# Expert results scattered to two DRAM rows per token, large tiles on multiples of 512 bytes, and a 4 KB descriptor ring

## The chip, the cores and the metric

The kernel runs on one core of a Trainium2 chip. The metric is the device time of one execution in microseconds. Three runs of the kernel before took 1555.31, 1557.9 and 1559.6 us, median 1557.9. A core has five engines that matter here: TensorE (PE; its weight loads are PEld), VectorE (DVE), ScalarE (ACT), GpSimd (POOL) and SyncE (SP), and 16 DMA engines that all queues share. SP and ACT issue plain transfers, GpSimd the indirect ones.

## The reference

Two transformer blocks run one after the other on x of 512 tokens by 1024. The first has a chunked mLSTM beside a convolution branch (glu) and a gated feed-forward net; the second has latent attention and retention, cross attention on a memory, and a mixture of 32 experts, which is what the change is about:

```python
hm = rms_norm_2(x, moe_norm_g)
g_sel = argmax(hm @ w_group + b_group)                 # one group of 8 experts per token
_, top_idx = lax.top_k(e_logits + e_bias, 2)           # two experts of it
act = silu(hm @ w_gate[e]) * (hm @ w_up[e]) * gate[:, e]
x = x + sum over e of act @ w_down[e]                  # gate is zero but for the two experts
```

Every token so has a first and a second expert, and 512 tokens make 1024 pieces of work. Each expert has 3 MB of weights (1024 x 512 and 256 x 1024 in float32), 100 MB in all.

## The kernel before

The phases follow each other, and a scheduler moves instructions of later phases ahead on each engine: mem (memory projections), glu, qk and vo with the mLSTM, wout, up and down (the feed-forward net), mlain, g, ret and att (second block), wout2, crossq, wo, and moe. A product in float32 is made of three matmuls on split operands (L146 to L148). Weight pieces of 512 KB come by SP into `raw` tiles (three buffers) and are split by ACT and DVE into `whl` tiles (four) (L131 to L141).

**The expert loop.** The 32 experts run as 16 pairs, p and p+16: the slots of the first are partitions 0 to 63, those of the second 64 to 127. So there are 2048 slots for 1024 pieces of work. `look` turns a pair's one-hot `oh` into the token of each slot and its gates by four small matmuls on `parts`; `fetch` (L1818) gathers the tokens' rows from `hd` in DRAM by an indirect DMA that drops unused slots; `pair_flip` (L1771) transposes them to `xT`; `pair_up` makes 16 matmuls (L1880), silu on ACT (L1882) and the product `sl` on DVE (L1883); `pair_turn` transposes `sl` to `aT` (L1891, L1893); `pair_down` (L1906) gives the result, which ACT and DVE copy into `yt` (L1912); `pair_scatter` (L1916) is an indirect DMA of GpSimd that adds `yt`'s 128 rows to `sums` in DRAM; unused slots go to spare rows at its end. `sums` was filled with x ahead of the loop (L1623, eight DMAs of ACT). After the loop SP reads `sums` into `xs` (tiles `crossq_U`, L1713), pair 15 is added by matmuls (`pair_last`, L1947, L1948) and SP stores the output (L1949, eight DMAs of 256 KB).

**The places.** The weights of the experts are 192 pieces of 512 KB (12 a pair). They are loaded by SP (L1755) into a ring of places, tiles that have become free: eight `ew`, four rows of X, two of `misc`, three `raw`, four `whl` twice, four rows of a U tile twice, and at last the four tiles of `xs`, 37 in all. Piece n goes to place n modulo 37 and so waits for piece n-37 to be used. The last four pieces are loaded as eight halves (L1749).

Of the kernel before, what the change touches and what calls it, by code (L numbers as in the profile page):

```python
# [46 lines left out]
class Kern:  # L47
# [15 lines left out]
    def setup(self):  # L63
# [11 lines left out]
        nc.vector.memset(self.half, -0.5)  # L75

# [419 lines left out]
    def block1(self):  # L496
# [47 lines left out]
        with tc.tile_pool(name="pf", bufs=1) as pf:  # L544
# [20 lines left out]
            self.rope_tables()  # L565
            g2row = self.mod_row(pf.tile([P, 1024], F32, tag="row1", name="g2row"), 2, 1, "ffn_post_g")
# [14 lines left out]
            for self.later in self.wide_product(act, "ffn_down", NFF, (((0, 1), 0, 8), ((0,), 8, 22), ((1,), 8, 22)),  # L581
                                                self.post(g2row, after)):
                pass

# [182 lines left out]
    def gate_cols(self, pa, gi, B, M):  # L767
# [6 lines left out]
        ac = pa.tile([P, 32], F32, tag="acol", name="acol")  # L774
        nc.vector.tensor_copy(ac, pt[:, :32])
# [216 lines left out]
    def attention(self, p2):  # L992
# [12 lines left out]
        sspe = p2.tile([P, 4], F32, tag="sspe", name="sspe")  # L1005

# [470 lines left out]
    def select_tiles(self, pm):  # L1477
# [3 lines left out]
        self.sel = {"oh": T("goh", 4), "o1": T("go1", 4, 8), "o2": T("go2", 4, 8), "mask": T("mask", 32), "mb": T("mb", 32, dt=BF16)}  # L1481
        self.pos = T("pos", 32)

    def select(self, pm, lg, br, t0, n):
# [19 lines left out]
        for dst in (s["mb"], s["mask"]):  # L1504
            nc.vector.tensor_tensor(dst[:, t].rearrange("p t (g e) -> p t g e", g=4), ob, ohb, op=ALU.mult)
# [51 lines left out]
    def moe(self, pm, o, X):  # L1557
# [27 lines left out]
        self.sums = self.dr.tile([S + P, D], F32, tag="sums", name="sums")  # L1585

# [6 lines left out]
        self.spare = pm.tile([P, 1], F32, tag="spare", name="spare")  # L1593
        nc.gpsimd.iota(self.spare, pattern=[[1, 1]], base=S - 1024, channel_multiplier=1, allow_small_or_imprecise_dtypes=True)
# [4 lines left out]
        def logits(tb, h):  # L1599
# [23 lines left out]
            nc.scalar.dma_start(self.sums[tb * P:(tb + 1) * P, c], x)  # L1623
# [23 lines left out]
        self.pieces = []  # L1647
# [5 lines left out]
        def route(tbs):  # L1653
            self.places_of(tbs)
            t = slice(tbs[0], tbs[-1] + 1)
            self.slots(oh[:, t], self.pair_pos(0)[:, t])
# [26 lines left out]
        for p in range(3):  # L1683
            st[p] = st.get(p, {})
            st[p]["oh"] = self.slots(self.slot_tile(), self.pair_pos(p))
# [5 lines left out]
        for p in range(3):  # L1691
            self.pair_gates(st[p], self.look(st[p]["oh"], self.parts), (p, p + 16, 32))
        nwin = self.more_windows(pm, mb, onb)

        xs = self.xs
        self.places += xs
        self.prefetch(0)
        yt = pm.tile([P, 2, 1024], F32, tag="y", name="yt")
        for i in range(16):
# [5 lines left out]
            if i + 3 < 16:  # L1705
                p = i + 3
                st[p] = self.pair_take(self.pair_pos(p), self.parts, (p, p + 16, 32))
# [13 lines left out]
    def places_early(self, X):  # L1721

        t = self.pm.tile([P, self.EXTRA, 1024], F32, tag="ew", name="ew")
        self.places = [t[:, i] for i in range(self.EXTRA)] + [X.rows(4 + i) for i in range(4)]
# [53 lines left out]
    def pair_pos(self, p):  # L1778

        return self.pos.rearrange("p t (j e) -> p t e j", j=2)[:, :, p]  # L1780
# [20 lines left out]
    def look(self, oh, parts):  # L1801
# [3 lines left out]
        o = ps[:, 0:3 * n].rearrange("p (n i) -> p n i", i=3)  # L1805
        for tb in range(4):
            self.nc.tensor.matmul(o, oh[:, tb].rearrange("p a b -> p (a b)"), parts[:, tb], start=tb == 0, stop=tb == 3)
# [13 lines left out]
    def pair_gates(self, s, ps, cols):  # L1821
# [8 lines left out]
        nc.vector.tensor_tensor(gt[:, 0:1], gt[:, 0:1], gt[:, 2:3], op=ALU.mult)  # L1830

        e = self.small(1)
# [5 lines left out]
    def pair_take(self, pos, parts, cols):  # L1838
# [306 lines left out]
```

## Time and profile before

| what | us |
|---|---|
| median of three runs | 1557.9 |
| lowest, highest | 1555.31, 1559.6 |
| profiled execution | 1556.0 |
| its span | 1554.3 |
| TensorE busy in the span | 1475.9 (95%) |
| VectorE, ScalarE, GpSimd busy | 947.2, 671.3, 132.4 |

Three kinds of view are used. The windows give the busy time of each engine in a stretch, the clock of TensorE and the share in which the 16 DMA engines had packets under way. The chain of waits leads from the last instruction back to what released each. The DMA view gives bytes, queues and the time from issue to landing of a stretch. A matmul's duration is longer than the distance from one to the next, since they overlap.

### The profile page before, as it was taken

The numbers are of one execution on the slowest core, as the hardware profiler recorded it, in microseconds if no ns is written. First come the engines' busy times: TensorE is split into PE (matmuls) and PEld (weight loads), VectorE is DVE, ScalarE is ACT, GpSimd is POOL, SyncE is SP. The second block draws the span as 40 slices with busy tenths as digits, with TensorE's granted clock in tenths as the row PEclk, the third lists the DMA queues.
The fourth block names the chain that finished last, engine by engine and source line by source line (L and its number), as shares of the span: only waits on it lengthen the run. The fifth ranks groups of instructions, "written<-read, shape, count | busy, mean of one in ns | idle before, by whom it ended". The sixth has DMA issues, their size and how long they took to land.

```text
span 1554.3 us, 19779 instructions
## 1 busy us (share of the span) xinstructions
PE 1475.9 (95%) x7032; PEld 1084.6 (70%) x7032; DVE 947.2 (61%) x2090; ACT 671.3 (43%) x1212; POOL 132.4 (9%) x153
## 2 busy tenths in 40 slices
PE   7989999999999999999999999999998999998886
PEld 4667778778888888888888877778877873332322
DVE  4568999985856865656525778766587565321112
ACT  4554586567746644444324554444355321110000
POOL 0111111011000000000000010100010002221100
PEclk9999999999999999999999999999999999999999
DMA  8899977876376433333435633342352689999997
GB/s 318 301 267 261 266 198 189 241 180 150 97 273 198 137 109 95 93 91 93 144 108 180 204 115 100 124 140 72 116 181 110 255 330 338 376 376 389 384 383 289
DMA packets 94470, 321.38 MB, mean 207 GB/s; under 512 B 12026, under 2 KB 12538, under 8 KB 94368
## 3 DMA queue, kind: packets, MB, share of 16 engines
q1 hardware_dynamic: 78384, 270.10, 50.1%
q0 software_dynamic: 11952, 39.49, 12.1%
q10 hardware_dynamic: 4032, 10.49, 1.8%
q8 instruction: 57, 0.93, 0.2%
q14 instruction: 45, 0.37, 0.1%
HBM read 273.74 MB, written 24.64 MB: 192 GB/s over the span
## 4 chain that ended last, share of the span: by engine, by line
PE 67%; DMA 16%; DVE 10%; ACT 2%; issue 2%; POOL 2%; SPq 0%; DVEq 0%; ACTq 0%; POOLq 0%
PE up_pa L148 5%; PE up_pa L147 5%; PE up_pa L146 5%; DMA ew<-in_w_gu_dram 3%; PE moe_pa L1880 2%; DVE y L632 2%; PE vo_pa L146 2%; PE vo_pa L148 2%; PE vo_pa L147 2%; PE wout_pa L148 2%; DMA moe_ew<-in_w_gu_dram 2%; PE wout_pa L146 2%; PE wout_pa L147 2%; DMA glu_raw<-in_w_in_dram 2%; DMA crossq_U<-in_w_dn_dram 2%
## 5 line engine op out<-in xcount | busy, mean ns | idle before, releaser
L632 DVE SCALAR_TENSOR_TENSOR y<-g,cols,y 128x493 f32<-128x493 f32 (+26 forms) x240 | 165.6, 727 | 6.6 <-ACT y L629 4.9
L148 PE MATMUL up_pa<-u,up_w 128*128 128x512 f32 (+1 forms) x384 | 145.6, 380 | 0.0
L147 PE MATMUL up_pa<-u,up_w 128*128 128x512 f32 (+1 forms) x384 | 144.1, 376 | 0.5 <-DVE u L189 0.5
L146 PE MATMUL up_pa<-u,up_w 128*128 128x512 f32 (+1 forms) x384 | 144.3, 377 | 0.0
L919 DVE SCALAR_TENSOR_TENSOR up_tA<-up_pa,cols,up_tA 128x511 f32<-128x511 f32 x88 | 65.8, 748 | 78.7 <-ACT up_tA L917 77.3
L1772 DVE COPY moe_xT<-moe_pb 128x512 f32<-128x512 f32 x15 | 10.4, 692 | 124.3 <-PE moe_pa L1880 122.8
L147 PEld LDWEIGHTS up_pa<-u,up_w 128*128 128x128 f32 x384 | 72.1, 188 | 16.6 <-DVE u L189 0.8
L146 PEld LDWEIGHTS up_pa<-u,up_w 128*128 128x128 f32 x384 | 72.4, 189 | 15.2 <-ACT u L188 0.5
L148 PEld LDWEIGHTS up_pa<-u,up_w 128*128 128x128 f32 x384 | 72.2, 188 | 13.8
L141 DVE TENSOR_TENSOR down_w<-down_raw,down_w 128x1024 fp32r<-128x1024 f32 x36 | 42.7, 1219 | 56.0 <-ACT down_w L135 56.0
L141 DVE TENSOR_TENSOR wout_w<-wout_raw,wout_w 128x512 fp32r<-128x512 f32 (+1 forms) x72 | 51.3, 745 | 35.2 <-ACT wout_w L135 35.1
L1882 ACT ACTIVATE moe_sl<-moe_pa,moe_gt 128x256 f32<-128x256 f32 x16 | 7.6, 473 | 141.6 <-PE moe_pa L1880 141.6
L917 ACT ACTIVATE up_tA<-up_pa,cols 128x512 f32<-128x512 f32 x44 | 34.2, 778 | 73.4 <-PE up_pa L148 73.4
L135 ACT CAST down_w<-down_raw 128x1024 fp32r<-128x1024 f32 x36 | 36.6, 1050 | 64.9 <-PE down_pb L148 31.9
L135 ACT CAST wout_w<-wout_raw 128x512 fp32r<-128x512 f32 (+1 forms) x72 | 44.9, 670 | 44.3 <-PE wout_pa L148 22.0
L146 PE MATMUL glu_pa<-mem_U,glu_w 128*128 128x512 f32 x128 | 51.1, 402 | 4.4 <-ACT mem_U L188 4.4
L141 DVE TENSOR_TENSOR up_w<-up_raw,up_w 128x1024 fp32r<-128x1024 f32 (+1 forms) x48 | 54.0, 1126 | 0.1
L147 PE MATMUL g_pa<-g_w,down_U 128*128 128x512 f32 x128 | 51.0, 398 | 0.5 <-DVE g_w L141 0.5
L146 PE MATMUL g_pa<-g_w,down_U 128*128 128x512 f32 x128 | 51.4, 402 | 0.0
L147 PE MATMUL glu_pa<-mem_U,glu_w 128*128 128x512 f32 x128 | 50.5, 396 | 0.4 <-DVE mem_U L189 0.4
L148 PE MATMUL g_pa<-g_w,down_U 128*128 128x512 f32 x128 | 50.7, 396 | 0.0
L148 PE MATMUL glu_pa<-mem_U,glu_w 128*128 128x512 f32 x128 | 50.4, 395 | 0.0
(749 smaller groups left out, 3944.4 us busy)
## 6 DMA issues: line engine op xcount, KB each, us to landing
up_raw<-in_ffn_up_dram SPq DMA_DIRECT2D x44, 512.0 KB, 3.5
wout_raw<-in_w_out_dram SPq DMA_DIRECT2D x40, 512.0 KB, 4.2
down_raw<-in_ffn_down_dram SPq DMA_DIRECT2D x36, 512.0 KB, 3.7
ew<-in_w_gu_dram SPq DMA_DIRECT2D x33, 512.0 KB, 10.0
glu_U<-in_ada_w_dram SPq DMA_DIRECT2D x32, 512.0 KB, 8.1
crossq_U<-in_w_gu_dram SPq DMA_DIRECT2D x24, 512.0 KB, 12.3
moe_ew<-in_w_gu_dram SPq DMA_DIRECT2D x19, 512.0 KB, 13.2
mem_raw<-in_w_kv_dram SPq DMA_DIRECT2D x16, 512.0 KB, 6.1
```

The lines of the kernel that those rows point to most:

```text
L135: nc.scalar.copy(w[:, 0, c], raw[:, c])
L141: nc.vector.tensor_tensor(w[:, 1, c], raw[:, c], w[:, 0, c].bitcast(F32), op=ALU.subtract)
L146: mm(out, lh, rh, start=start, stop=False)
L147: mm(out, lh, rl, start=False, stop=False)
L148: mm(out, ll, rh, start=False, stop=stop)
L632: nc.vector.scalar_tensor_tensor(acc[:, s:], g[:, :512 - s], cw[:, j:j + 1], acc[:, s:], op0=ALU.mult, op1=ALU.add)
L917: nc.scalar.activation(acc, pq, AF.Identity, scale=cwv(2), bias=self.col("ffn_conv_b", cc))
L919: nc.vector.scalar_tensor_tensor(acc[:, s:], pq[:, :512 - s], cwv(2 - s), acc[:, s:], op0=ALU.mult, op1=ALU.add)
L1772: (nc.scalar.copy if i else nc.vector.tensor_copy)(t[:, i * 4:i * 4 + 4].rearrange("p k c -> p (k c)"), ps)
L1880: nc.tensor.matmul(ps[r, :], s["xT"][:, k, r], w[j][k // 2][:, (k % 2) * 512:(k % 2 + 1) * 512], start=k == 0, stop=k == 7)
L1882: nc.scalar.activation(sl, ps[:, :256], AF.Silu, scale=s["gt"][:, 2:3])
```

## The change

It has five parts.

- The scatter no longer adds. Each pair's `yt` goes to `rows`, 1024 rows of 4 KB: row t for a token's first expert, row 512 + t for its second. Unused slots are dropped. To know which it is, `select` keeps a one-hot `second`, and `look` multiplies it with `oh` in four more matmuls. Pair 15 is added by matmuls as before.
- `clear_rows` writes zeros to all of `rows`: one memset and 16 DMAs of 256 KB on SP. They are placed in the up phase.
- x is no longer written to `sums`; it stays in `xs`, whose tiles are no places any more. A new tile `early` gives two places that are filled in glu. So there are 35.
- After pair 14 ACT issues eight DMAs of 512 KB that read `rows` into places, and eight adds of 128x1024 on VectorE add them to `xs`.
- Unused tiles (`gap0`, `gapa`, `gap2`, `gap`) are put between tiles so that large ones start at a multiple of 512 bytes in a partition; the ring of descriptors for GpSimd's DMAs goes from 16 to 4 KB a partition, which makes the room. Of the tiles in the prediction `u`, `up_act` and `mT` move from 352 past a multiple to a multiple; `ew` starts off one before (352) and after (480); the U tiles, `raw` and `whl` tiles are on one in both.

```diff
+        self.p0.tile([P, 112], F32, tag="gap0", name="gap0")
...
             self.rope_tables()
+            self.clear_rows()
...
+        self.rows = self.dr.tile([2 * S, D], F32, tag="rows", name="rows")
+        z = self.tB()
+        nc.vector.memset(z, 0.0)
+        for i in range(8):
+            for h in range(2):
+                nc.sync.dma_start(self.rows[i * P:(i + 1) * P, h * 512:(h + 1) * 512], z)
...
+        early = self.p0.tile([P, 2, 1024], F32, tag="early", name="early")
+        self.pieces, self.places = [], [early[:, 0], early[:, 1]]
+        self.prefetch(0)
...
-        for dst in (s["mb"], s["mask"]):
-            nc.vector.tensor_tensor(dst[:, t].rearrange("p t (g e) -> p t g e", g=4), ob, ohb, op=ALU.mult)
+        for dst, v in (("mb", ob), ("mask", ob), ("second", o2)):
+            nc.vector.tensor_tensor(s[dst][:, t].rearrange("p t (g e) -> p t g e", g=4), v, ohb, op=ALU.mult)
...
-            nc.scalar.dma_start(self.sums[tb * P:(tb + 1) * P, c], x)
...
-        self.places += xs
-        self.prefetch(0)
...
+            if i == 14:
+                n = len(self.places)
+                for tb in range(4):
+                    for k in range(2):
+                        z = self.places[(192 + 2 * tb + k) % n]
+                        nc.scalar.dma_start(z, self.rows[k * S + tb * P:k * S + (tb + 1) * P, :])
         for tb in range(4):
-            nc.sync.dma_start(xs[tb], self.sums[tb * P:(tb + 1) * P, :])
+            for k in range(2):
+                z = self.places[(192 + 2 * tb + k) % n]
+                nc.vector.tensor_tensor(self.xs[tb], self.xs[tb], z, op=ALU.add)
...
+        if p is not None:
+            self.second = ps[:, 3 * n:3 * n + 2]
+            for tb in range(4):
+                self.nc.tensor.matmul(self.second, ohs[tb], self.both(self.sel["second"], p)[:, tb], start=tb == 0, stop=tb == 3)
...
-        nc.vector.tensor_scalar(e, gt[:, 1:2], 0.0, self.spare, op0=ALU.is_equal, op1=ALU.mult)
-        nc.vector.tensor_tensor(to, gt[:, 1:2], e, op=ALU.add)
+        for j in range(2):
+            r = slice(64 * j, 64 * j + 64)
+            nc.vector.tensor_scalar(to[r], self.second[r, j:j + 1], float(S), gt[r, 1:2], op0=ALU.mult, op1=ALU.add)
...
-        self.nc.gpsimd.indirect_dma_start(out=self.sums, out_offset=bass.IndirectOffsetOnAxis(ap=s["to"], axis=0), in_=y,
-                                          in_offset=None, bounds_check=S + P - 1, compute_op=ALU.add)
+        self.nc.gpsimd.indirect_dma_start(out=self.rows, out_offset=bass.IndirectOffsetOnAxis(ap=s["to"], axis=0), in_=y,
+                                          in_offset=None, bounds_check=2 * S - 1, oob_is_err=False)
...
-    nc = _bacc.Bacc("TRN2", target_bir_lowering=False, num_devices=1)
+    nc = _bacc.Bacc("TRN2", target_bir_lowering=False, num_devices=1, dynamic_dma_scratch_size=4096)
```

The change moves instructions at three places that matter. The first is VectorE at the end of the loop, here in the kernel before; `yt` is pair 14's result, the rows behind it are pair 15's:

```order
L1912 COPY yt<-moe_pa_12490 128x512
L1883 SCALAR_TENSOR_TENSOR moe_sl_12521<-moe_sl_12521,moe_gt_12365,moe_pa_12504 128x256
L1893 COPY moe_aT_12527<-moe_pa_12524 128x256
L189 TENSOR_TENSOR moe_y_12533<-moe_pa_12534,moe_y_12533 128x512
L1948 TENSOR_TENSOR crossq_U_10345<-crossq_U_10345,moe_pb_12543 128x512
L189 TENSOR_TENSOR moe_y_12533<-moe_pa_12563,moe_y_12533 128x512
L1948 TENSOR_TENSOR crossq_U_10345<-crossq_U_10345,moe_pb_12548 128x512
```

And in the kernel after, where `wo_raw`, `wo_ew` and `wo_U` are the places into which `rows` is read:

```order
L1941 COPY yt<-moe_pa_12557 128x512
L1736 TENSOR_TENSOR crossq_U_10373<-crossq_U_10373,wo_raw_10754 128x1024
L1736 TENSOR_TENSOR crossq_U_10373<-crossq_U_10373,wo_raw_10755 128x1024
L1736 TENSOR_TENSOR crossq_U_10373<-crossq_U_10373,wo_ew_10756 128x1024 x2
L1736 TENSOR_TENSOR crossq_U_10373<-crossq_U_10373,wo_ew_10757 128x1024 x2
L1736 TENSOR_TENSOR crossq_U_10373<-crossq_U_10373,wo_U_10758 128x1024
L1912 SCALAR_TENSOR_TENSOR moe_sl_12596<-moe_sl_12596,moe_gt_12432,moe_pa_12579 128x256
L1736 TENSOR_TENSOR crossq_U_10373<-crossq_U_10373,wo_U_10758 128x1024
L1922 COPY moe_aT_12602<-moe_pa_12599 128x256
L194 TENSOR_TENSOR moe_y_12612<-moe_pa_12613,moe_y_12612 128x512
L1977 TENSOR_TENSOR crossq_U_10373<-crossq_U_10373,moe_pb_12622 128x512
```

Seven of the eight adds stand ahead of pair 15's `sl`, one between it and `aT`; behind the first `y` come four adds of pair 15 (one of them shown) where there was one, and four behind the second.

The second place is ScalarE at the same point, in the kernel after:

```order
L1941 COPY yt<-moe_pa_12556 128x512
L1732 DMA wo_raw_10754<-rows 128x1024
L1732 DMA wo_raw_10755<-rows 128x1024
L1732 DMA wo_ew_10756<-rows 128x1024 x2
L1732 DMA wo_ew_10757<-rows 128x1024 x2
L1732 DMA wo_U_10758<-rows 128x1024 x2
L1911 ACTIVATE moe_sl_12596<-moe_pa_12579,moe_gt_12432 128x256
L193 CAST moe_y_12612<-moe_pa_12613 128x512
```

In the kernel before the silu `moe_sl` followed the copy to `yt` but for one copy of `xT`; now the eight DMA issues are between the two.

The third place is SP in the up phase, in the kernel after; `rows` are the clears:

```order
L136 DMA up_raw_4828<-in_ffn_up_dram 128x1024
L972 DMA down_sm_6204<-in_pos_dram 128x4
L976 DMA down_tB_6208<-in_inv_freq_dram 128x96
L1778 DMA misc<-in_w_gu_dram 128x1024
L599 DMA rows<-down_tB_6228 128x512 x6
L136 DMA up_raw_4858<-in_ffn_up_dram 128x1024
L599 DMA rows<-down_tB_6228 128x512
L136 DMA up_raw_4900<-in_ffn_up_dram 128x1024
L599 DMA rows<-down_tB_6228 128x512
```

The loads of `up_raw` kept their order; ten more clears follow between the next ones.

## Rows read from the trace of the kernel before

**Rows 1.** The page: busy tenths in 40 slices of 38.9 us.
```profile
PE   7989999999999999999999999999998999998886
...
DMA  8899977876376433333435633342352689999997
```

**Rows 2.** Windows: stretch, length, busy us of PE, PEld, DVE, ACT, POOL, clock, DMA share, GB/s.
```profile
80.00:90.00 10.00, 5.69 (x22) 4.08 (x23) 7.23 (x15) 6.01 (x10) 1.93 (x4) 1.00 1.03 299
90.00:200.00 110.00, 110.00 (x500) 83.42 (x499) 95.03 (x144) 53.29 (x61) 15.27 (x18) 0.98 0.99 264
500.00:766.00 266.00, 262.46 (x1209) 214.00 (x1208) 168.42 (x242) 123.18 (x176) 2.56 (x4) 0.99 0.34 102
766.00:872.00 106.00, 106.00 (x474) 87.52 (x473) 48.85 (x60) 37.77 (x48) 1.39 (x2) 1.00 0.52 173
1300.00:1380.00 80.00, 76.78 (x394) 29.36 (x392) 24.99 (x89) 9.79 (x19) 17.15 (x14) 1.00 1.02 364
1380.00:1520.00 140.00, 116.61 (x458) 40.54 (x455) 23.64 (x78) 11.68 (x23) 17.78 (x13) 0.96 1.03 387
```

**Rows 3.** Chain of waits, 1500 to 1554.3: start, us, what.
```profile
1519.38 10.90 DMA ew<-in_w_gu_dram
...
1532.80 0.49 DVE moe_sl L1883
```

**Rows 4.** DMA, 1400 to 1440: GB/s per 1 us; GpSimd's queue (packets, MB); a gather's landing.
```profile
GB/s 262 266 287 348 418 418 422 426 418 414 422 422 422 422 418 406 422 410 393 401 254 262 283 340 410 414 426 410 430 414 414 422 422 422 414 418 418 414 430 410
...
q0 software_dynamic: 560, 1.52, 15.9%
...
moe_xg<-hd,moe_sm POOLq DMA_INDIRECT x2, 7.0
```

**Rows 5.** Timeline of GpSimd: start us, us, instruction, idle before it.
```profile
1302.98 1.62 POOL L1916 DMA_INDIRECT sums<-yt,moe_sm  x1 [1.70 <-DVE moe_sm L1836]
...
1315.86 1.59 POOL L1916 DMA_INDIRECT sums<-yt,moe_sm  x1 [4.16 <-DVE yt L1912]
...
1415.01 1.59 POOL L1916 DMA_INDIRECT sums<-yt,moe_sm  x1 [4.14 <-ACT yt L1912]
...
1523.77 1.55 POOL L1916 DMA_INDIRECT sums<-yt,moe_sm  x1 [16.99 <-DMA ew<-in_w_gu_dram]
```

**Rows 6.** The tail: issues, landing, and durations, by timeline, tile, line and DMA view.
```profile
1520.55 10.12 SPq L1749 DMA_DIRECT2D ew<-in_w_dn_dram  x8
...
ew<-in_w_dn_dram SPq DMA_DIRECT2D x1, 256.0 KB, 6.7
...
L141 DVE TENSOR_TENSOR wo_w<-wo_raw,wo_w 128x1024 fp32r<-128x1024 f32 x8 | 9.8, 1222 | 8.2 <-ACT wo_w L135 8.2
...
1542.27 4.58 DVE L1948 TENSOR_TENSOR crossq_U<-crossq_U,moe_pb 128x512 f32<-128x512 f32 x7
...
1542.41 2.84 PE L1947 MATMUL moe_pb<-moe_y,moe_back 128*128 128x512 f32 x7 [0.23 <-DVE moe_y L189]
...
DMA to landing us min/median/max: 2.0/4.2/4.9
```

**Rows 7.** Matmuls of up and down by shape: count, busy us, mean ns, idle before.
```profile
L148 PE MATMUL up_pa<-u,up_w 128*128 128x512 f32 x320 | 127.7, 399 | 0.0
...
L146 PE MATMUL up_pa<-u,up_w 128*128 128x512 f32 x320 | 125.4, 392 | 0.0
...
L148 PE MATMUL down_pa<-down_w,up_U 128*128 128x512 f32 x64 | 24.9, 389 | 0.0
...
L146 PE MATMUL down_pa<-down_w,up_act 128*128 128x512 f32 x24 | 9.5, 396 | 0.0
```

**Rows 8.** ScalarE's waits, 78 to 205, and the landing of `up_raw` (min, median, max).
```profile
ACT glu_w L135 <- DMA glu_raw<-in_w_in_dram: 27.7, 10, 5.7
...
DMA to landing us min/median/max: 3.4/3.5/5.7
```

**Rows 9.** The small matmul of the lookups, 1280 to 1540, by shape.
```profile
L1807 PE MATMUL moe_pb<-parts,moe_oh 128*128 128x3 bf16 x8 | 0.3, 164 | 0.0
```

More of the change, by code (lines that the diff above doesn't have):

```diff
@@ L75, in setup @@
         nc.vector.memset(self.half, -0.5)
+        self.p0.tile([P, 8], F32, tag="mcol", bufs=2, name="mcol")
+        self.p0.tile([P, 8], F32, tag="cvec", name="cvec")
+        self.p0.tile([P, 8], F32, tag="cond", name="cond")
+        self.p0.tile([P, 112], F32, tag="gap0", name="gap0")
     def col(self, name, i=0, n=1):
@@ L1479, in T @@
             return pm.tile([P, 4, *sh], dt, tag=nm, name=nm)
-        self.sel = {"oh": T("goh", 4), "o1": T("go1", 4, 8), "o2": T("go2", 4, 8), "mask": T("mask", 32), "mb": T("mb", 32, dt=BF16)}
+        self.sel = {"oh": T("goh", 4), "o1": T("go1", 4, 8), "o2": T("go2", 4, 8), "mask": T("mask", 32), "mb": T("mb", 32, dt=BF16), "second": T("second", 32, dt=BF16)}
         self.pos = T("pos", 32)
@@ L1655, in route @@
             t = slice(tbs[0], tbs[-1] + 1)
-            self.slots(oh[:, t], self.pair_pos(0)[:, t])
+            self.slots(oh[:, t], self.both(self.pos, 0)[:, t])
         rest = Halves([])
@@ L1684, in moe @@
             st[p] = st.get(p, {})
-            st[p]["oh"] = self.slots(self.slot_tile(), self.pair_pos(p))
+            st[p]["oh"] = self.slots(self.slot_tile(), self.both(pos, p))
             if p:
@@ L1706, in moe @@
                 p = i + 3
-                st[p] = self.pair_take(self.pair_pos(p), self.parts, (p, p + 16, 32))
+                st[p] = self.pair_take(self.both(pos, p), self.parts, (p, p + 16, 32), p)
             if i < 15:
@@ L1723, in places_early @@
         t = self.pm.tile([P, self.EXTRA, 1024], F32, tag="ew", name="ew")
-        self.places = [t[:, i] for i in range(self.EXTRA)] + [X.rows(4 + i) for i in range(4)]
+        self.places += [t[:, i] for i in range(self.EXTRA)] + [X.rows(4 + i) for i in range(4)]
         self.places += [self.misc[:, :1024], self.misc[:, 1024:]]
@@ L1776, in slot_tile, with both @@
         return self.p0.tile([P, 4, 2, 64], BF16, tag="tB", bufs=4, name=self.nm("oh"))
-    def pair_pos(self, p):
-        return self.pos.rearrange("p t (j e) -> p t e j", j=2)[:, :, p]
+    def both(self, v, p):
+        return v.rearrange("p t (j e) -> p t e j", j=2)[:, :, p]
     def slots(self, oh, pos):
@@ L1805, in look @@
         o = ps[:, 0:3 * n].rearrange("p (n i) -> p n i", i=3)
+        ohs = [oh[:, tb].rearrange("p a b -> p (a b)") for tb in range(4)]
         for tb in range(4):
-            self.nc.tensor.matmul(o, oh[:, tb].rearrange("p a b -> p (a b)"), parts[:, tb], start=tb == 0, stop=tb == 3)
+            self.nc.tensor.matmul(o, ohs[tb], parts[:, tb], start=tb == 0, stop=tb == 3)
+        if p is not None:
+            self.second = ps[:, 3 * n:3 * n + 2]
+            for tb in range(4):
+                self.nc.tensor.matmul(self.second, ohs[tb], self.both(self.sel["second"], p)[:, tb], start=tb == 0, stop=tb == 3)
         return o
@@ L1978, in overflow @@
             for p in range(16):
-                nc.vector.tensor_copy(st[:, :, 0:2], self.pair_pos(p))
-                nc.vector.tensor_copy(st[:, :, 2:4], self.info[:, :, 0:32].rearrange("p t (j e) -> p t e j", j=2)[:, :, p])
+                nc.vector.tensor_copy(st[:, :, 0:2], self.both(self.pos, p))
+                nc.vector.tensor_copy(st[:, :, 2:4], self.both(self.info[:, :, 0:32], p))
                 nc.vector.tensor_copy(st[:, :, 4:6], self.info[:, :, 32:34])
```

19 lines of the change are left out of this document (9 added, 10 removed).

## The prediction

> **What bounds the kernel now.** I read the page's forty slices first [rows 1]: TensorE's digit is 8 or 9 in all but the first and the last slice, while the DMA digit is high at two places, the first eight slices and the last eight. The windows by stage [rows 2] sharpen that. In the up and down products TensorE is busy 262.5 of 266 us and 106 of 106, with the DMA engines at 0.34 and 0.52: there only a shorter matmul helps. From 1300 to 1520 the DMA share is 1.02 and 1.03, and from 1380 TensorE has time to spare (116.6 of 140 us). The chain of waits leads over weight pieces, the last of them 10.9 us from issue to landing [rows 3]. So the expert loop lives on the weight stream.
>
> What holds that stream back is seen in slices of 1 us [rows 4]: it runs at 410 to 430 GB/s, and twice for four slices at 254 to 340. Each dip comes some 5 us after a scatter-add left GpSimd [rows 5] (at 1415.01, the dip from 1420; the first dip belongs to the scatter before the window). The gathers (two of them in the same window) leave no dip. There are 15 scatter-adds, one for each pair 0 to 14. The first 80 us of the loop TensorE is nearly full (76.8 of 80); it then uses up the lead of 37 loaded places and falls behind the stream.
>
> **The scatter.** In one dip the four slices 254, 262, 283, 340 move 1.14 MB; at 418 GB/s they would move 1.67, so 0.53 MB or 1.27 us is lost, and the scatter's own 128 rows of 4 KB (0.52 MB) take another 1.25 us: 2.5 us of the stream for each. After, unused slots are dropped, as the gather drops them already. The tokens fill 1024 of the 2048 slots, so 64 rows or 0.26 MB on average; the rows bear it out: two gathers and two scatter-adds move 1.52 MB [rows 4], less 2 x 0.52, which is 0.24 MB per gather. Priced like a gather, with no dip, that is 0.26/0.418 = 0.6 us. Saving 1.9 us each. The bounds: 0.6 if only the bytes go and the dip stays, 1.9 if both go. I take 1.9, since the gather is the nearest row (same engine, same descriptors of 4 KB, same row list). Until scatter 14 is issued there are 14 of them: 26.6 us. Two fewer places (35 for 37) mean that two more pieces of 512 KB are loaded inside the bound stretch: 2 x 1.25 = 2.5 us. Scatter 14 leaves at 1523.8 now [rows 5], and 24.1 us earlier after: 1499.7 on the old scale. TensorE allows it: 12.8 us lie between the scatter-adds at its own pace (1302.98 to 1315.86 [rows 5]), 14 of which end at 1482.
>
> **The tail, where part of it is given back.** Before, pair 15 doesn't depend on the scatters until its last adds; SP reads back 2 MB. After, ACT issues eight reads of 512 KB that wait for scatter 14, and pair 15's silu stands behind them; VectorE has seven adds of 128x1024 in front of pair 15's product `sl`, each waiting for one read. Scatter 14 lands a gather's 7.0 us after its issue [rows 4]: 1506.7. ACT's eight issues are short beside the reads themselves and lie ahead of their landing. The last half piece of w_dn lands at about 1537.0 now (issued by 1530.3, 6.7 us) [rows 6] and at 1537.0 - 24.1 - 1.9 = 1511.0 after, so 4.3 us of weights still share the engines with 4.2 MB of reads (10.0 us): the eighth read lands near 1521.0, the seventh near 1519.8. An add of this size takes 1.22 us [rows 6], about as long as a read, so the adds keep up, and the seventh ends near 1521.0. `sl` of pair 15 then starts at 1521.1 against 1532.8 [rows 3]: 11.7 us ahead, so 12.4 of the 24.1 are given back. The eighth add stands between `sl` and the copy of `aT`; half a microsecond of it lies beside TensorE's transpose: +0.7. At the end something is won. Now seven adds of pair 15 run after the second half's y (1542.27, 4.58 us [rows 6]) and six of eight output DMAs queue behind each other; after, four adds of the first half go ahead of the second half's y and only four come behind it. TensorE's last products end at 1545.3 [rows 6] on that scale, so the last add ends 0.9 us earlier, and the last store finds a shorter queue (landing 2.0 us at best, 4.9 at worst [rows 6]): together 2.5 us, bounds 0.9 and 3.8. Tail and loop: -11.7 + 0.7 - 2.5 = -13.5 us.
>
> **The alignment.** In the program of before, `u`, `up_act` and `mT` start 352 bytes past a multiple of 512; the gaps put them on one. In one phase, with the same weights' tiles, the down product shows both cases [rows 7]: 389 ns for a matmul on `up_U` (on a multiple), 396 on `up_act` (six lines of 24); the up product on `u` 392 to 399. The up product has 960 of them, three lines of 320 of which the first and the last stand here (the middle one is 394, their mean 395). 960 x 6 ns + 144 x 7 ns = 6.8 us, in stages where TensorE hardly waits. `mT`'s stage waits for DMA, so nothing. The bounds: 0, if something else in those products makes them slow, and 6.8. I take 6.8, since the two cases of the down product differ in that operand alone. The Trainium skill, "SBUF — State Buffer", Operand start alignment, asks only that an operand start at a multiple of its element size, and calls that a matter of legality, not of speed: by that rule alone the gaps would give nothing, and the sum would be 6.8 us less.
>
> **The rest.** The two early pieces are loaded between those of glu, where the DMA engines are at 0.99 to 1.03 and ACT waits 27.7 us in all for such loads [rows 2, 8]. At 264 GB/s one is 2.0 us. The first falls at 80 to 90 us, where TensorE waits (5.7 of 10 busy): +2.0. The second falls where it is full: nothing. Bounds 0 and 4. Clearing 4.2 MB costs 10 us of DMA in a stage that uses 0.34 of it [rows 2]. Six of them (1.6 MB, 3.8 us) stand ahead of one `up_raw`, which lands in 3.5 us otherwise [rows 8]; three raw buffers at 24 matmuls each (5.5 us) give it 11 us, so nothing. Without that cover it would be 4 us. VectorE's memset is one instruction with SP's first six clears behind it; it stands ahead of the conversion for which the next load on SP waits anyway. The lookup of first or second choice adds four matmuls and four weight loads a pair; in the loop TensorE has room, and for the three lookups ahead of it 12 matmuls are added on 2 columns, of which the nearest (3 columns) takes 164 ns [rows 9]: 2.0 us if nothing overlaps, nothing if they fill its waits; I take 0.6, since they follow twelve of their kind and overlap. The 2 MB of `sums` written ahead of the loop go: nothing to -2, taken as nothing, since TensorE bounds there. The ring of 4 KB costs GpSimd nothing by the rows: it is idle over 4 us ahead of a scatter-add in the loop [rows 5]. No row shows a ring that is full.
>
> **Sum.** -13.5 - 6.8 + 2.0 + 0.6 = -17.7 us. The profiled execution took 1556.0 us (span 1554.3): 1538.3. The median of the runs stands 1.9 above it: 1540.2.
>
> **Rivals.**
> First, a plain scatter holds the stream nearly as long as one with add. For it: the rows show no plain write by row list, and the dip could be the writes to scattered rows rather than the add. Against it: the gather reads by the same list without a dip, and the stores of the output land in 2.0 us. With s the saving for each, all 15 count: 1540.2 + 15 x (1.9 - s). At s = 0.6 (only bytes) it is 1560, at 0, 1569. It is slower than before from s below 0.7.
> Second, the tail is dearer: the reads arrive in a bunch, because they share all engines, and the seven adds then run one after the other, 8.5 us after the last. Scale: +7.3, 1547.5. For it: loads in the stream take 11 us [rows 3] where one alone takes 3.5 [rows 8], so many are under way. Against: the queue's rate of 418 GB/s is that of one piece after the other, 1.25 us each.
> Third, alignment gives nothing, since the products on `u` and `up_act` are slower for another reason (their operands are written by other engines and later): 1547. Against it stand [rows 7]. This is the outcome that the Trainium skill's rule on operand starts, cited above, would lead to.
> Fourth, the front pays: glu's loads 4 instead of 2, and the clears hold up one `up_raw` by 4: 1546.
> Fifth, the change doesn't do what it says in the tail, because reads and adds are hidden better than I have it (the reads take the place of w_dn without delay): 1535.
>
> **How the numbers follow.** A measurement of this kernel can tell some 0.3% or 4.7 us from no change, so "same" is 1553.2 to 1562.6. Chances: the forecast 0.54, the scatter 0.15, the tail 0.10, alignment 0.11, front 0.06, cheaper tail 0.04. All but the first rival are faster alone, some not when they meet; of the first 0.10 lies above 1562.6 and 0.05 within. Faster 0.81, same 0.09, slower 0.10. The range reaches from 1531 (saving of sums' traffic and the better end) to 1557.
>
> **What would show it.** In the new profile: no dip below 380 GB/s in the loop; scatter landing near 7 us; a matmul of `up_pa` at 389 ns; ACT's reads right after scatter 14; VectorE's `sl` of pair 15 some 14 us behind scatter 14's landing. Dips that stay after each scatter make the prediction wrong first; a TensorE share near 1 in the loop would be the next.

## The result, and the profile after

The kernel after takes 1543.28 us (median of four runs, 1540.46 to 1545.11), the kernel before 1557.36 beside it: a ratio of 0.9908 with a 95% interval of 0.9886 to 0.9929, some 14 us less. The forecast was 1540.2, range 1531 to 1557. Its profiled execution, the fastest of the four, took 1540.46 us with a span of 1538.7, 15.6 us under the span before.

The page after, first the span, then busy tenths in 40 slices, answers to [rows 1]:

```profile
span 1538.7 us, 19919 instructions
...
PE   7999999999999999999999999999999999999883
...
PEclk9999999999999999999999999999999999999997
DMA  9999977876385553333436542342352678999995
```

The shape is the same. New are the last slices: TensorE falls to 8 and 3, and its granted clock to 0.7 in the last one.

Four marks cut the difference into pieces. The forecast's share of each is in the last column.

| piece, before and after in us from the start | before | after | difference | forecast |
|---|---|---|---|---|
| start to scatter 0 | 1302.98 | 1293.23 | -9.75 | -4.2 |
| scatter 0 to scatter 14 | 220.8 | 199.9 | -20.9 | -24.1 |
| scatter 14 to pair 15's `sl` | 9.0 | 22.9 | +13.8 | +12.4 |
| `sl` to the end | 21.5 | 22.8 | +1.3 | -1.8 |
| span | 1554.3 | 1538.7 | -15.6 | -17.7 |

**The up stage.** The matmuls of `up_pa` before, after, and in the run with alignment alone (e4_align, below): minimum, median and maximum ns, and first and last start.

```profile
L146 PE MATMUL up_pa<-u,up_w x384: 278/392/1202, 509.1 to 765.6; 128*128 128x512 f32 x160, 128*128 128x256 f32 x32
...
L148 PE MATMUL up_pa<-u,up_w x384: 278/399/399, 509.3 to 766.0; 128*128 128x512 f32 x160, 128*128 128x256 f32 x32
```

```profile
L151 PE MATMUL up_pa<-u,up_w x384: 274/389/480, 504.8 to 753.9; 128*128 128x512 f32 x160, 128*128 128x256 f32 x32
...
L153 PE MATMUL up_pa<-u,up_w x384: 278/389/389, 505.0 to 754.3; 128*128 128x512 f32 x160, 128*128 128x256 f32 x32
```

```profile
L151 PE MATMUL up_pa<-u,up_w x384: 277/389/1202, 513.4 to 762.4; 128*128 128x512 f32 x160, 128*128 128x256 f32 x32
...
L153 PE MATMUL up_pa<-u,up_w x384: 279/389/389, 513.6 to 762.9; 128*128 128x512 f32 x160, 128*128 128x256 f32 x32
```

The medians stand at 389 ns after. From first start to last the stage takes 256.9 us before, 249.5 after and 249.5 with alignment alone: 7.4 us less, and the clears that lie in it after cost nothing that can be seen. The trace before has the longest of these stages. In the other four traces without the unused tiles (e1, e2, e3, e11) it takes 254.6 to 256.1 us, in the nine with them 248.2 to 249.9, and the two means lie some 6.5 us apart.

**The stream.** The same 40 us as in [rows 4], after: GB/s in slices of 1 us, and GpSimd's queue.

```profile
GB/s 422 393 422 414 401 393 360 397 426 393 418 410 418 422 414 418 418 406 422 406 414 381 352 430 414 385 426 414 410 401 373 418 418 410 426 369 414 418 393 422
...
q0 software_dynamic: 720, 1.31, 8.6%
```

The dips to 254 are gone. What is left are single slices at 352 to 385, four of them under the 380 that the prediction named as its sign. Three gathers and two scatters moved 1.31 MB, 0.26 each, as the 64 rows of a mean pair make.

**The tail.** Chain of waits after, from scatter 14 on (start, us, what), then VectorE's timeline:

```profile
1493.08 6.59 DMA rows<-yt,moe_sm
...
1501.03 6.63 DMA wo_ew<-rows
...
1507.68 7.10 DMA wo_U<-rows
...
1514.80 1.23 DVE crossq_U L1736
1516.02 0.40 DVE moe_sl L1912
...
1518.37 5.19 PE moe_pa L1935 x10
```

```profile
1514.80 1.23 DVE L1736 TENSOR_TENSOR crossq_U<-crossq_U,wo_U 128x1024 f32<-128x1024 f32 x1 [2.44 <-DMA wo_U<-rows]
1515.94 0.47 DVE L1912 SCALAR_TENSOR_TENSOR moe_sl<-moe_sl,moe_gt,moe_pa 128x256 f32<-128x256 f32 x1
```

The chain is the forecast one: the scatter lands in 6.6 us, ScalarE's reads follow, the seventh lands 21.7 us after scatter 14 left (forecast 20.1), and its add is in front of `sl`. ScalarE's last two reads left only at 1507.68, when an earlier read had landed; I put the 1.6 us down to that, and no run shows it apart.

The stream under that chain was not the forecast one. The sum had the engines full with weights and reads from the scatter's landing on. But of SyncE's eight halves of w_dn one left at 1495.07 and the other seven from 1504.61 to 1511.5, three of them behind the last read. Meanwhile the stream ran at 242 GB/s from 1496 to 1499 and at 154 from 1499 to 1502. SyncE's longest wait from 1485 on for one of these halves (us in total, times, longest):

```profile
SPq L1772 <- DMA wo_raw<-rows: 9.2, 1, 9.2
```

That the seventh read lands so near the forecast is in part luck: the stream lost time at first, and weights that came late left some of it to the reads.

TensorE meanwhile had nothing to do, and its clock shows it (us, busy time of PE, PEld, DVE, ACT and POOL, granted clock, DMA share, GB/s):

```profile
1500.00:1505.00 5.00, 1.83 (x6) 0.37 (x6) 1.58 (x2) 0.00 (x0) 0.00 (x0) 1.00 0.80 292
1505.00:1510.00 5.00, 0.00 (x0) 0.00 (x0) 4.17 (x4) 0.47 (x1) 0.00 (x0) 0.62 0.98 376
1510.00:1515.00 5.00, 0.00 (x0) 0.00 (x0) 1.81 (x3) 0.00 (x0) 0.00 (x0) 0.50 1.04 364
...
1520.00:1525.00 5.00, 5.00 (x14) 1.77 (x10) 0.95 (x2) 0.59 (x1) 0.00 (x0) 0.67 0.00 0
```

With TensorE idle the granted clock went to 0.50, the lower of its two levels, 1.2 GHz. Ten matmuls of pair 15's down product then took 5.19 us where they took 2.76 before. The same matmuls in the chain of the kernel before, and the window around them:

```profile
1534.34 2.76 PE moe_pa L1906 x10
...
1535.00:1540.00 5.00, 5.00 (x21) 2.14 (x18) 1.38 (x2) 0.58 (x1) 0.00 (x0) 1.00 0.97 348
```

### The profile page after: what moved, and what is told of

Same layout as the page of the kernel before. It is cut to its first block, busy times and chain, and to the rows that moved or that the text cites. A ratio compares the mean times of both kernels' runs of the same rounds, so it can differ in the third digit from the quotient of the medians.

```text
span 1538.7 us, 19919 instructions
## 1 busy us (share of the span) xinstructions
PE 1458.5 (95%) x7096; PEld 1082.9 (70%) x7096; DVE 960.3 (62%) x2101; ACT 671.2 (44%) x1212; POOL 124.5 (8%) x152
## 3 DMA queue, kind: packets, MB, share of 16 engines
q0 software_dynamic: 11952, 35.56, 10.4%
## 4 chain that ended last, share of the span: by engine, by line
PE 68%; DMA 14%; DVE 9%; issue 3%; ACT 3%; POOL 2%; SPq 0%; ACTq 0%; POOLq 0%; DVEq 0%
PE up_pa L152 5%; PE up_pa L153 5%; PE up_pa L151 5%; PE moe_pa L1909 4%; PE moe_pa L1935 3%; DMA glu_w<-glu_raw 3%; PE vo_pa L151 2%; DMA glu_raw<-in_w_in_dram 2%; PE vo_pa L153 2%; PE vo_pa L152 2%; PE wout_pa L153 2%; PE wout_pa L151 2%; PE wout_pa L152 2%; PE qk_pa L153 1%; PE qk_pa L151 1%
## 5 line engine op out<-in xcount | busy, mean ns | idle before, releaser
L152 PE MATMUL up_pa<-u,up_w 128*128 128x512 f32 (+1 forms) x384 | 142.6, 372 | 1.0 <-DVE u L194 1.0
L153 PE MATMUL up_pa<-u,up_w 128*128 128x512 f32 (+1 forms) x384 | 142.5, 372 | 0.0
L151 PE MATMUL up_pa<-u,up_w 128*128 128x512 f32 (+1 forms) x384 | 142.4, 372 | 0.0
```

The lines of the kernel that those rows point to most:

```text
L151: mm(out, lh, rh, start=start, stop=False)
L152: mm(out, lh, rl, start=False, stop=False)
L153: mm(out, ll, rh, start=False, stop=stop)
```

## The experiments

Theory and rivals are those of the prediction, taken one by one. All times are medians with the kernel before in the same job (1557.38 us for the first four, 1558.29 for the next four, 1554.67 for e9 and e10, 1558.15 for the last two). The ratios leave out the profiled execution, so they can lie some 2 us beside the quotient of two medians.

### The scatter: add, rows, or both

e1_plain, on the kernel before:

```diff
-                                          in_offset=None, bounds_check=S + P - 1, compute_op=ALU.add)
+                                          in_offset=None, bounds_check=S + P - 1)
```

> Kernel before with one thing changed: the scatter into sums no longer adds (a plain write of all 128 rows, spare rows included; a token's row in sums then holds one expert's result instead of the sum). Theory of the prediction: of the 2.5 us that each scatter-add takes from the weight stream 1.27 us are the dip (the add), 1.25 us its bytes. Then the dips to 254-340 GB/s go, the bytes stay, and 14 scatters give 14 x 1.27 = 18 us: about 1539 us. Rival: the dip belongs to writing to scattered rows, not to the add: dips stay, 1557 us.

1537.64 us, ratio 0.9874 (0.9853 to 0.9895): 19.7 us less. The same 40 us of its stream:

```profile
GB/s 426 410 422 406 418 414 393 393 410 410 426 422 414 414 410 426 414 418 418 406 418 406 418 434 406 422 422 414 434 410 418 426 410 434 418 406 422 418 430 418
```

No dip is left. The dip was the add, and its price was right: 18 us were forecast for 14 scatters, and the interval is 16.4 to 22.9. From scatter 0 to pair 15's `sl` the trace is 18.5 us shorter than before (211.3 against 229.8).

e2_drop, on the kernel before, the add kept:

```diff
-        e = self.small(1)
-        nc.vector.tensor_scalar(e, gt[:, 1:2], 0.0, self.spare, op0=ALU.is_equal, op1=ALU.mult)
...
-        nc.vector.tensor_tensor(to, gt[:, 1:2], e, op=ALU.add)
+        nc.vector.tensor_copy(to, gt[:, 1:2])
...
-                                          in_offset=None, bounds_check=S + P - 1, compute_op=ALU.add)
+                                          in_offset=None, bounds_check=S - 1, oob_is_err=False, compute_op=ALU.add)
```

> Kernel before with the add kept, but unused slots dropped instead of being sent to spare rows (64 rows in the mean instead of 128). Theory: the bytes halve, 0.6 us each, and the dip too if it is paid by the row: 14 x 1.25 = 17.5 us, about 1540 us, dips half as long. Rival a: the dip is paid by the transfer, only bytes go: 14 x 0.6 = 9 us, 1548 us. Rival b: dropped rows cost as much as written ones: 1557 us.

1546.8 us, ratio 0.9918 (0.9896 to 0.994): 10.6 us less, near the 9 of rival a, far from 17.5, and the interval (9.3 to 16.2) holds neither. The dips stay, shorter and at 283 to 353:

```profile
GB/s 283 402 418 373 430 414 414 389 410 422 410 410 316 283 353 389 401 365 414 410 385 406 422 406 414 410 410 422 418 422 393 324 311 394 414 356 348 393 328 406
```

The dips did shrink, so it is not rival a's mechanism either. Against 418 GB/s, nine slices from 3 us after each scatter lose 1.3 us before, 0.9 in the mean here, and nothing in e1 (estimates from the slices of 1300 to 1500). A third of the dip goes with half of the rows.

e3_plain_drop has both edits.

> Kernel before with both: no add and unused slots dropped, so the scatter of the kernel after with the old places, the old tail and the old alignment (a token's row in sums holds one expert's result instead of the sum). Theory: 14 x 1.9 = 26.6 us, about 1531 us, as nothing else of the change is there. Rival: TensorE's own pace of 12.8 us a pair, or the chain by pair, becomes the bound before all is won: 1535 to 1540 us.

1534.02 us, ratio 0.9858 (0.9831 to 0.9885): 23.4 us less, and not 26.6. By the medians, dropping the unused rows so gave 3.6 us on top of e1, where their bytes by the stream's rate are worth 14 x 0.6 = 8.8. The intervals of e1 and e3 overlap, so 3.6 is not clear of nothing; by the traces it is 1.0 us up to scatter 14 (201.0 and 200.0 from scatter 0) and 4.9 up to pair 15's `sl` (211.3 and 206.3). Its stream, and then the line of GpSimd's queue over the whole execution from the page of e1 (packets, MB):

```profile
GB/s 406 401 422 410 418 414 414 414 410 381 410 385 402 426 385 434 397 422 422 406 422 414 406 406 410 414 426 410 414 377 369 389 414 422 414 406 410 414 414 414
```

```profile
q0 software_dynamic: 11952, 39.49, 11.0%
```

The same line from the page of e3:

```profile
q0 software_dynamic: 11952, 35.56, 10.5%
```

There are slices at 369 to 402 again. The queue moved 3.93 MB less, some 960 rows of 4 KB, but it has the same 11952 packets, and the page counts 12985 packets under 512 B where that of e1 counts 12026, some 960 more: a dropped row is still a (small) packet, and the queue's time fell only from 11.0% to 10.5%. The windows from 1380 to 1500 show the loss, e1 first (the last two figures are DMA share and GB/s):

```profile
1380.00:1500.00 120.00, 105.86 (x452) 37.75 (x448) 23.83 (x79) 12.21 (x24) 12.24 (x12) 0.99 1.03 418
...
1380.00:1500.00 120.00, 104.89 (x460) 38.15 (x458) 22.45 (x73) 11.71 (x23) 13.09 (x13) 0.99 1.02 409
```

With the engines as full as in e1 the stream moved 9 GB/s less, which in 120 us is 2.6 us of it. That the dropped rows take this time is how I read it; no run measured a dropped row alone. The rival, TensorE's pace, doesn't fit: its share was 105 of 120 us from 1380 on.

### Alignment, and the ring

e4_align, on the kernel before (and, not shown, two more unused tiles and three small ones taken earlier, so that every other large tile lies where the kernel after has it):

```diff
+        self.p0.tile([P, 112], F32, tag="gap0", name="gap0")
...
+        pa.tile([P, 96], F32, tag="gap", name="gapa")
...
+        p2.tile([P, 120], F32, tag="gap", name="gap2")
...
-    nc = _bacc.Bacc("TRN2", target_bir_lowering=False, num_devices=1)
+    nc = _bacc.Bacc("TRN2", target_bir_lowering=False, num_devices=1, dynamic_dma_scratch_size=4096)
```

> Kernel before with only the unused tiles and the 4 KB ring of the change (same order of instructions on each engine, large tiles on multiples of 512 bytes, ew left where it was). Theory of the prediction: up and down products at 389 ns, 6.8 us less, 1550.5 us. Rival from the trace after: the stages of mem and glu are shorter too by 3 to 4 us because of alignment, so 11 us less, 1546 us. Rival: the gain in those early stages has another cause (early loads, another order), then mem keeps its length.

1548.24 us, ratio 0.9931 (0.991 to 0.9952): 9.1 us less by the medians, between 7.5 and 14 by the ratio. The up stage gives 7.4 of it (rows above; 6.5 in the means of all traces). The mem stage gives next to nothing: its last product starts at 77.5 us, at 77.8 in the kernel before.

e11_ring, the last two lines of that diff alone:

> Kernel before with the 4 KB descriptor ring alone: same order of instructions, same tiles' offsets to 512 bytes. Theory: the ring costs and gives nothing, 1557 us, and the 9 us of the run with ring and unused tiles are the alignment's. Rival: the smaller ring holds up GpSimd's indirect transfers (their issue or landing is later): slower than before.

1557.54 us, ratio 1.0002 (0.9983 to 1.002). The ring costs and gives nothing, and the 9 us come with the unused tiles. Which multiple matters no run tells: 352 bytes are off 64, 128 and 256 as well.

e12_ew is e7_tail_sp (below) with one more tile:

```diff
+        self.pm.tile([P, 8], F32, tag="gapm", name="gapm")
         t = self.pm.tile([P, self.EXTRA, 1024], F32, tag="ew", name="ew")
```

> The kernel whose SyncE reads the rows behind w_dn and whose adds stand behind pair 15's y, with one more unused tile of 32 bytes that puts the eight ew places on a multiple of 512 bytes as well (480 past one in the kernel after). Theory: alignment speeds TensorE's operands in stages that TensorE bounds; the expert loop is bound by the stream, so nothing beyond 1 us: 1533 us. Rival: transfers into places off a multiple are slower too, some 6% for each of the 45 of 192 pieces that go to ew, 3 us: 1530 us.

1533.71 us, ratio 0.9852 (0.9829 to 0.9876), against 0.9851 without. In the loop the eight `ew` places gain nothing. The medians alone could not settle the rival's 3 us; the traces do: scatter 0 to 14 takes 199.1 us here and 199.4 in e7. Nor did TensorE's matmuls of pairs on `ew` (128*64, 128x512) change: their means are 596 and 600 ns in both.

### The tail

e5_tail, on the kernel after:

```diff
-            if i == 14:
-                n = len(self.places)
-                for tb in range(4):
-                    for k in range(2):
-                        z = self.places[(192 + 2 * tb + k) % n]
-                        nc.scalar.dma_start(z, self.rows[k * S + tb * P:k * S + (tb + 1) * P, :])
-        for tb in range(4):
-            for k in range(2):
-                z = self.places[(192 + 2 * tb + k) % n]
-                nc.vector.tensor_tensor(self.xs[tb], self.xs[tb], z, op=ALU.add)
+        n = len(self.places)
+        with self.tc.issue_after(st[15]["silu"].ins):
+            for tb in range(4):
+                for k in range(2):
+                    z = self.places[(192 + 2 * tb + k) % n]
+                    nc.scalar.dma_start(z, self.rows[k * S + tb * P:k * S + (tb + 1) * P, :])
         for h in range(2):
             self.pair_down(st[15], self.pair_weights(15), (h,))
-            self.pair_last(st[15], h)
+        with self.tc.issue_after(self.last.ins):
+            for tb in range(4):
+                for k in range(2):
+                    z = self.places[(192 + 2 * tb + k) % n]
+                    nc.vector.tensor_tensor(self.xs[tb], self.xs[tb], z, op=ALU.add)
+                for h in range(2):
+                    self.pair_last(st[15], h, (tb,))
...
```

> Kernel after with only the order of its tail changed: ScalarE issues the eight reads behind pair 15's silu, and VectorE's eight adds stand behind pair 15's two y, by token block, each followed by that block's last adds and stores. Theory: what the tail gives back (sl of pair 15 starts at 1515.9, though its up product ended at 1501.9) is that order alone; with pair 15 first sl starts near 1502.4, the reads still end near 1516, the last adds 2 to 3 us later, the stores 4 us after them: span near 1524, 14 us less than the kernel after, about 1529 us. Rival: the 4.2 MB of reads after scatter 14 bound the tail in any order, and the work behind them is as long as now: 1538 to 1543 us.

1535.2 us, ratio 0.9862 (0.984 to 0.9884): 8 us under the kernel after. The order was most of what the tail gave back, but 14 us were not to be had.

e7_tail_sp, here against e5, with the eight reads on SyncE:

```diff
-        with self.tc.issue_after(st[15]["silu"].ins):
...
-                    nc.scalar.dma_start(z, self.rows[k * S + tb * P:k * S + (tb + 1) * P, :])
+                nc.sync.dma_start(z, self.rows[k * S + tb * P:k * S + (tb + 1) * P, :])
```

> As the one before with the changed tail, but SyncE issues the eight reads, behind the last halves of w_dn. Theory: in the kernel after SyncE's halves of w_dn were issued only from 1504.6 on, while ScalarE's reads had been queued, and the DMA engines stood at 0.59 to 0.74 from 1490 to 1500; with one queue the halves go first, and y of pair 15 is not behind the issues on ScalarE: 1 to 4 us less than with ScalarE's reads, 1525 to 1528 us. Rival: the stream after scatter 14 bounds both alike, no difference.

1533.73 us, ratio 0.9851 (0.9831 to 0.9872): the fastest here with e12, 9.5 us under the kernel after. The forecast of 1525 to 1528 was missed by 6. Against e5 the difference lies within the intervals, so the rival (no difference) stands. VectorE's timeline in it (start, us, instruction, idle before it) shows the new bound:

```profile
1502.77 0.48 DVE L1912 SCALAR_TENSOR_TENSOR moe_sl<-moe_sl,moe_gt,moe_pa 128x256 f32<-128x256 f32 x1 [10.09 <-ACT moe_sl L1911]
...
1509.63 2.48 DVE L1737 TENSOR_TENSOR crossq_U<-crossq_U,wo_raw 128x1024 f32<-128x1024 f32 x2
1512.21 1.29 DVE L1977 TENSOR_TENSOR crossq_U<-crossq_U,moe_pb 128x512 f32<-128x512 f32 x2
1513.41 3.61 DVE L1737 TENSOR_TENSOR crossq_U<-crossq_U,wo_ew 128x1024 f32<-128x1024 f32 x3
...
1521.60 1.22 DVE L1737 TENSOR_TENSOR crossq_U<-crossq_U,wo_U 128x1024 f32<-128x1024 f32 x1
1522.93 1.28 DVE L1977 TENSOR_TENSOR crossq_U<-crossq_U,moe_pb 128x512 f32<-128x512 f32 x2
```

`sl` starts at 1502.77, as expected, 13 us earlier than in the kernel after. From 1509.63 to 1524.21 VectorE then has no idle time that a transfer ended: eight adds of 1.22 and eight of 0.65 one behind the other. In the kernel after the adds of the rows ran in the shadow of the reads; moved behind pair 15 most of them have no cover. e5's forecast had the reads end near 1516, the last add near 1519 and the span near 1524. Here the last add ends at 1524.2, which is 5 us of what was missing, and the span at 1531.6: the stores behind it take 7.4 us instead of 4 to 5.

e10_split_adds, here against e7, lets TensorE add every second read, by a matmul with the identity into pair 15's bank:

```diff
-                nc.tensor.matmul(pc, back[:, tb * P:(tb + 1) * P], y[:, i, c], start=i == 0, stop=i == 1)
+                nc.tensor.matmul(pc, back[:, tb * P:(tb + 1) * P], y[:, i, c], start=i == 0, stop=False)
+            nc.tensor.matmul(pc, self.ident, z[:, c], start=False, stop=True)
...
```

> As the kernel whose SyncE reads the rows behind w_dn and whose adds stand behind pair 15's y, but the second of the two reads of each token block is added by TensorE (a matmul with the identity into the bank that pair 15's result is summed in) instead of by VectorE. In that kernel VectorE was busy without a gap from 1509.6 to 1524.2. Theory: four adds of 1.22 us less on it, 4.9 us less at most; the reads end near 1515 and bound what is left: 1529 to 1531 us. Rival: TensorE's eight matmuls of 0.9 us at full clock (twice that at half) take the place of the adds: 1534 us or more.

1536.22 us, ratio 0.9885 (0.9869 to 0.9902), no better than e7: the rival. By the traces, too, `sl` to the end takes 28.0 us (1505.06 to 1533.1) where e7 takes 28.8. TensorE is full from 1515 to 1520 and VectorE waits 3.2 us for it. Part of that is the clock: it was granted at 0.77 from 1510 to 1515 and at 0.89 from 1515 to 1520. The first and the last group of these matmuls on TensorE, then VectorE's wait:

```profile
1514.40 2.72 PE L1976 MATMUL moe_pb<-wo_raw,ident 128*128 128x512 f32 x4
...
1522.92 1.88 PE L1976 MATMUL moe_pb<-wo_U,ident 128*128 128x512 f32 x4
```

```profile
1516.30 0.69 DVE L1977 TENSOR_TENSOR crossq_U<-crossq_U,moe_pb 128x512 f32<-128x512 f32 x1 [3.17 <-PE moe_pb L1976]
```

### The clock

e6_warm, on the kernel after (e9_warm18 has 18 for 12):

```diff
+            if i == 15:
+                with self.tc.issue_after(st[15]["mm"].ins):
+                    dd = self.psB()
+                    for _ in range(12):
+                        warm = nc.tensor.matmul(dd, self.ident, self.cols[:, :512], start=True, stop=True)
+                with self.tc.issue_after(warm.ins):
+                    self.pair_turn(st[i])
```

> Kernel after with twelve matmuls of 128x512 on constants put on TensorE between pair 15's up product and its transposes, where it idles 14.6 us; their result is used by nothing. Theory: the granted clock falls to 0.5 in that idle stretch and the ten matmuls behind it take 5.2 us instead of 2.8 as in the kernel before; kept busy it stays at 1.00 and the tail is 2.5 to 3 us shorter, about 1540.5 us. Rival: those matmuls are slow for another reason (places just read into), the time stays at 1543.

1543.86 us, ratio 0.9912 (0.989 to 0.9934). It decided nothing: the twelve ended 6.6 us before the transposes, and the clock was 0.50 again from 1520 to 1525. Pair 15's transposes with the idle time before them:

```profile
1520.76 0.69 PE L1928 MATMUL moe_pa<-ident,moe_sl 128*128 128x128 f32 x2 [6.58 <-DVE moe_sl L1920]
```

> As the kernel with twelve matmuls on constants in TensorE's wait, but with eighteen. The twelve took 10.6 us and left 6.6 us idle, in which the clock fell again, so they decided nothing; eighteen take 15.9 of the 17.2 us. Theory: the clock is 1.00 when pair 15's transposes come, the ten matmuls behind take 2.8 us instead of 5.2, the stretch from sl of pair 15 to the end is 20 us instead of 22.8: about 1540.5 us. Rival: that stretch stays at 22 to 23 us with the clock at 1.00, because VectorE and the stores set it: 1543.

1542.01 us, ratio 0.9925 (0.9907 to 0.9943). By the medians no difference from the kernel after (0.9908). By its trace the theory holds: the clock stayed at 1.00 over pair 15's products, and the stretch from `sl` (1516.48) to the end (1537.1) takes 20.6 us instead of 22.8 (22.2 in e6, where the clock had fallen too). TensorE's windows (busy, clock, DMA share, GB/s), then `sl`:

```profile
1515.00:1520.00 5.00, 4.13 (x15) 1.00 0.55 217
1520.00:1525.00 5.00, 5.00 (x19) 1.00 0.12 48
...
1516.48 0.47 DVE L1920 SCALAR_TENSOR_TENSOR moe_sl<-moe_sl,moe_gt,moe_pa 128x256 f32<-128x256 f32 x1
```

That is 1.6 to 2.2 us, at most 0.14%, less than the medians of these runs can tell apart.

### Without the second row

e8_align_drop is e2 and e4 together on the kernel before: the scatter still adds.

> Kernel before with the unused tiles, the 4 KB ring and dropped unused slots, but the scatter still adds into sums: no second lookup, no clears, no eight reads and adds. By the runs of each alone (9.1 and 10.6 us less) the two add up to 19.7, about 1537.7 us, which would be 5 us under the kernel after. Rival: they share a bound (TensorE's pace in the loop is the same in both), 1541 us or more.

1539.06 us, ratio 0.9882 (0.986 to 0.9904): 19.2 us less by the medians, near the 19.7 of the two parts. The interval (1536.5 to 1543.3) holds the rival's 1541, too; the trace decides against a shared bound. The up stage takes 249.5 us as in e4, and scatter 0 to 14 takes 210.8 us, with 210.4 in e2 and 220.8 before. Its first and last scatter:

```profile
1296.35 1.62 POOL L1923 DMA_INDIRECT sums<-yt,moe_sm  x1 [2.13 <-DVE yt L1919]
...
1507.16 1.55 POOL L1923 DMA_INDIRECT sums<-yt,moe_sm  x1 [15.65 <-DMA ew<-in_w_gu_dram]
```

The interval of its ratio and the kernel after's (0.9886 to 0.9929) overlap at their edges. The largest part of the change, the second row per token with its clears, reads and adds, so didn't earn more than dropping unused slots under the old add, as long as the tail stood as it does in the kernel after. With the tail in the other order it does: beside e8 the four runs of e7 took 1533.36 to 1534.96 us, those of e8 1537.07 to 1540.24.

## Why the prediction was right, point by point

- **The bound.** Right. The expert loop is bound by the stream; e1 changed nothing but the kind of write and won 19.7 us.
- **The scatter, 1.9 us each.** The dip's term (18 us for 14) was right: 19.7. The term of the bytes was mis-sized: 0.6 each by the gather's bytes, 8.8 in all, and 3.6 by the medians of e1 and e3. Both together 23.4 (17.9 to 26.3) instead of 26.6. In the kernel after scatter 0 to 14 is 20.9 us shorter. It would be tempting to add the 2.5 for two more pieces and read 23.4 again, but e3, which keeps the 37 places, takes as long for that stretch (200.0 us, 199.9 after). So no run shows the 2.5. The first rival (the write is as dear without add) fell with e1.
- **Handing back in the tail, 12.4 us.** 13.8 in the trace. The step that was off by 1.4 is the seventh read (21.7 us behind the scatter's issue instead of 20.1). It came that near by luck in part, since SyncE's halves of w_dn left late, three of them behind the reads, for which the sum had no term. `sl` came 16.3 us behind the scatter's landing, with some 14 named as the sign. That it is the order and not the reads, e5 and e7 show: `sl` starts near 1502.9 in both.
- **The end, -1.8.** Wrong sign: +1.3. The step that failed is that the rows from `sl` on would keep their durations. TensorE waited 14.6 us ahead of them and ran at half clock; e9's trace gives 2.2 of the 3.1 us back (1.6 against e6). The rest stays open.
- **Alignment, 6.8 us.** Right. The prediction's 5.8 for the up stage is 7.4 by the two traces and 6.5 by the means of all, and the 144 matmuls on `up_act` went from 396 to 389 ns, which is its 1.0. For the kernel e4 gives 9.1 (7.5 to 14); what is above the stages' sum I can't place. The weighed rule of the Trainium skill, "SBUF — State Buffer", Operand start alignment, holds as far as it goes: it is about which starts are legal, and says itself that its runs timed nothing. Read as a rule on time it would be wrong here by 9 us.
- **The early loads, +2.0.** Wrong: glu takes hardly longer. Its first and last start are 81.0 and 181.6 before, 78.0 and 177.5 after; over seven traces each, with the loads and without, its mean length is 101.1 and 100.7 us, with a spread of up to 2.7. The loads found room although the DMA share was 0.99 to 1.03; the first left SyncE at 69.1 already, not at 80 to 90. The clears cost nothing, as forecast; 16 issues lay between 528.5 and 547.0 and the stage is as short as in e4. The lookups' 0.6 can't be told: from the last product of wo to scatter 0 the kernel after takes 36 us, e7 takes 35, the kernel before 35. In the loop they do show: where TensorE sets the pace the scatters lie 12.97 us apart instead of 12.81, and that is made up before scatter 14 (199.9 us after, 200.0 in e3).
- **What I had no term for.** The mem stage is 3.0 us shorter in the profile after. It is 1.4 and 1.6 shorter in e1 and e3 too, which have the front of the kernel before, and 0.4 in e4, which has the alignment. I take it for scatter between executions. The four runs of the kernel after lie 5 us apart, and in the other six traces with the same front mem's last product starts 0.5 to 1.8 us later than here. Over the seven of them scatter 0 leaves 8.0 us earlier than over the five with the front of before, so some 1.7 of the 9.75 in the table are this execution's.

Sum: loop and tail with the clock came out 7.6 us dearer than forecast, the front 5.5 us cheaper (3.8 in the means), so part of the nearness of 1540.2 and 1543.3 is luck: errors that cancel.

## What to carry to other kernels

Price a transfer by what it does to its neighbours: look at the stream's rate in slices of 1 us around it, and ask whether it is the operation or the bytes that dents it. When a write-and-add-later scheme takes the place of an accumulate, the adding has to be put where something covers it: here its order alone decided 8 us of a change worth 14. And a wait on TensorE of 14.6 us was paid twice here, once as waiting and once in the matmuls that came after it.

## What the runs showed of the hardware that I had not expected

- A matmul of 128x512 (128*128) in the up and down products whose operand starts 352 bytes past a multiple of 512 took 392 to 399 ns instead of 389, and the up stage 254.6 to 256.9 us instead of 248.2 to 249.9. It is no rule for every operand: pairs' matmuls (128*64) on `ew` took 596 and 600 ns whether `ew` lay 480 bytes off (e7) or on a multiple (e12), and transfers into it showed no price either. What makes the difference no run tells.
- An indirect DMA that adds 128 rows of 4 KB dents the stream beyond its bytes: 1.3 us each, gone in e1 when it only writes.
- Dropped slots seem cheaper than written ones but not free: 3.6 us won by the medians where their bytes are 8.8, and a stream of 409 GB/s for 418 at full engines; each is still a packet.
- TensorE's granted clock fell to 0.50 in an idle stretch of 14.6 us, and again in one of 6.6 us.
